# Hybrid attention and short-convolution layer: the last three product steps split by token block, one bias transfer and one power moved

## The chip, the cores and the metric

The kernel runs on one core of a Trainium2 chip. The metric is device time in microseconds (us), the median of three runs. Engines are named as in the profile: PE (matrix products) with PEld (its weight loads), DVE and ACT (elementwise), POOL (here powers and DMAs that add while they copy), SP (plain DMAs).

## The reference, cut to what matters

```python
h = rms_norm(x, norm_gain[i])
z = h @ w_in[i]                                  # q, k, v, gates, conv parts
...                                              # attention, short convolution
x = x + mix @ w_out[i]
gate = jax.nn.sigmoid(rms_norm(x, ple_gate_norm_gain[i]) @ w_ple_gate[i] + b_ple_gate[i])
e = rms_norm(p[i] @ w_ple_proj[i], ple_norm_gain[i])
x = x + gate * e
```

512 tokens, width 2048, all in float32. The change touches the end of the last line, the products of the gate before it, and two orders further ahead.

## The kernel before, in words

Almost every product is float32 made of two parts: `halves` (lines 198 to 200) splits an operand into a rounded part h (a cast on ACT, L199) and the rest l (a subtraction on DVE, L200), and a product is h by h, l by h and h by l. The seven large matrix products of the middle and the end (nine column groups of 1024) go by a scheme of seven instead of eight block products: sums of blocks of the weights (L185 to L191 on DVE, or L169 as an adding DMA from POOL) are multiplied with sums of blocks of the activations.

A group g has 28 steps (`PER`), listed in `steps`. A step (g, f, c) multiplies form f of the activations with one 128x2x512 piece of weights: 6 matmuls for token block t=0, then 6 for t=1 (`products`, called in `run_step`), each 128x128 by 128x512, into a PSUM accumulator "a", "b" or "c" that several forms share. In the last group (g=8) "a" is two single banks. Step numbers below count from 0 inside a group, so the last is 27. The split weights wh, wl live in three buffers: the cast for step s+3 can start when PE has left step s. PE runs its program in the order written; DVE, ACT, POOL and SP each run their own lists in order, and those lists come from two tables: `soon(before|after, step, fn)` in the grouped stages, and `at(tick, fn)` in the attention stage. An instruction that waits holds up all behind it on its engine.

In group 8 the last two steps were already reordered: t=0 of both, then `tail_work`, then t=1 of both (L246 to L254).

Three places matter here.

- **Attention stage** (125 to 263 us). `turn_q` transposes q and issues three small POOL DMAs (L810, L811, L813) that rearrange it for the scores matmuls (L829, L830, L832); the third waits for the first to land. `rstd_q` turns sums of squares into norms: one small DVE instruction (L585) and a power on POOL (L303). `take_e` stores e tiles (L913, POOL).
- **Group 1 into group 2** (350 to 370 us). `tap` multiplies a finished block z by a row of convolution weights (DVE, L1074) and stores it (POOL, L1075). Its z buffers are the four of the pool `quad`; group 2's first eviction (`first`, ACT, L320) takes one of them again, and the casts of group 2's weights are queued on ACT behind it.
- **Group 8** (822 us to the end), `gate_group(8)`. For a block (t, n) of 2x128 tokens by 512 columns: `take` copies the first accumulator, scaled, from PSUM (ACT, L1325); `add_b` adds the bias by a POOL DMA (L1328); `join` adds the second accumulator (DVE, L1333); then sigmoid (ACT, L1348), `times_e` (DVE, L1352), `add_x2` (POOL DMA, L1355) and `store`. Blocks (0,0) and (1,0) at the very end go by smaller pieces: `bias_first` puts the bias into PSUM ahead (L1340), `first_block` (L1431 and others) and `last_block` (L1422, L1412, L1416) finish them, with stores from SP (L1417).

```python
        if s == len(steps) - 2:
            tail_products.append(products)
            products(0)
        elif s == len(steps) - 1:
            products(0)
            for fn in tail_work:
                fn()
            tail_products[0](1)
            products(1)
```

Of the kernel before, what the change touches and what calls it, by code (L numbers as in the profile page):

```python
# [15 lines left out]
P = 128  # L16
T = 512
# [18 lines left out]
def hymba_layer(ctx: ExitStack, tc: tile.TileContext, io):  # L36
# [82 lines left out]
    def soon(table, s, fn, *args):  # L119
        table.setdefault(s, []).append((fn, args))  # L120
# [93 lines left out]
    def run_step(s, forms):  # L214
        g, f, c = steps[s]
        now[0] = s
        for fn, args in before.pop(s, ()):
            fn(*args)
        sums(s + (3 if g in LATE and s % PER < 8 else 4))
        prepare(s + 2)  # L220
        acc = {1: "a", 6: "a", 7: "a", 4: "a", 5: "b", 3: "b", 2: "c"}[f]
        start = f in (1, 5, 2)
        mine = [x for x in steps if x[:2] == (g, f)]
        first, last = c == mine[0][2], c == mine[-1][2]
        if start and first:
            if (g, acc) == (NG - 1, "a"):
                ps = [ps_t.tile([P, T], F32, name="pst") for _ in range(2)]
            else:
                ps = ps_abc[("abc".index(acc) + max(g - 1, 0)) % 3].tile([P, 2, T], F32, name="psp")
                if g >= NG - 2:  # L230
                    ps = [ps[:, b] for b in range(2)]
            psum[g, acc] = ps
        ps = psum[g, acc] if g >= NG - 2 else [psum[g, acc][:, b] for b in range(2)]
        wh, wl = weights[s]

        def products(t, f=f, c=c, wh=wh, wl=wl, first=first, last=last):
            for i in range(2):
                _, h, l = forms[2 * c + i][f]
                h, l = (a[:, t * P : (t + 1) * P] for a in (h, l))
                for n, (a, w) in enumerate(((h, wh), (l, wh), (h, wl))):  # L240
                    nc.tensor.matmul(  # L241
                        ps[t], a, w[:, i], start=start and first and i == 0 and n == 0,
                        stop=last and i == 1 and n == 2, skip_group_check=not start,
                    )

        if s == len(steps) - 2:  # L246
            tail_products.append(products)
            products(0)
        elif s == len(steps) - 1:
            products(0)  # L250
            for fn in tail_work:
                fn()
            tail_products[0](1)
            products(1)  # L254
        else:
            for t in range(2):
                products(t)
        if g in (0, 4, 6, 8):
            for i in range(2):
                for home in forms[2 * c + i][f][0]:  # L260
                    room[home] += 1
        while s in after:
            for fn, args in after.pop(s):
                fn(*args)
# [50 lines left out]
    def column(r, t, b):  # L315
        return r[:, 2 * t + b : 2 * t + b + 1]
# [288 lines left out]
    def rstd_q(t, n):  # L605
        blocks = slice(2 * t, 2 * t + 2)
        head_rstd(rq[t, n], eps_tok[:, blocks])
# [95 lines left out]
    def at(when, fn):  # L703
        later.append((when, len(later), fn))
# [28 lines left out]
    for b in range(NB):  # L733
        scale_k(b)

    for t in range(2):
        rope_q(t, 1)
        for b in range(2):
            at(9 + 2 * t + b, lambda t=t, b=b: square_q(t, 0, b, mtile))
        at(11 + 2 * t, lambda t=t: rstd_q(t, 0))  # L740
        at(14 + 3 * t, lambda t=t: rope_q(t, 0))
    mask = cw.tile([P, P], F32, name="mask", bufs=1)
    nc.gpsimd.dma_start(mask, io["mask"])
# [68 lines left out]
        turned[j, t, 0], turned[j, t, 1] = st, st2  # L812
        return lambda: nc.gpsimd.dma_start(st[HD:], low[:HD])  # L813

    turned, laid = {}, [None]

    def attention(j, n, when):

# [65 lines left out]

        if n % 2 == 0:
            at(when - 5, lambda: cell.update(last=turn_q(j, n // 2)))
            at(when - 4, lambda: cell["last"]())
        at(when, scores)
        at(when + 5, turn)
        at(when + 8, values)  # L890
# [160 lines left out]
    def square_group(g):  # L1051

        s0, q = g * PER, {}
        quarters(g, q, s0)

        def times(t, src):
            for b in range(2):
                stt(q[t, 0][:, b], src()[:, b], column(rx2_tok, t, b), q[t, 1][:, b], op0=ALU.mult, op1=ALU.mult)

        def last():  # L1060
            q[1, 0] = qtile("z")
            times(1, lambda: psum[g, "a"])

        taps = []

        def load_taps():
            for i in range(3):
                taps.append(itile("tap"))
                nc.sync.dma_start(taps[i], io["conv_rows"][i])

        def tap(i, t, home):

            out = q[home]
            tt(out, q[t, 0], taps[i].unsqueeze(1).broadcast_to([P, 2, T]), op=ALU.mult)  # L1074
            nc.gpsimd.dma_start(part(tap_dram[i].rearrange("(b p) n -> p b n", p=P), t, 0), out)  # L1075

        soon(after, s0 + 24, load_taps)
        soon(after, s0 + 27, times, 0, lambda: q[0, 0])
        soon(after, s0 + 28, last)
        for i, t, home, s in (  # L1080
            (2, 0, (0, 1), 28), (1, 0, (1, 1), 29), (0, 0, (0, 0), 30),
            (2, 1, (0, 1), 32), (1, 1, (0, 1), 36), (0, 1, (1, 0), 37),
        ):
            soon(after, s0 + s, tap, i, t, home)
# [228 lines left out]
    def gate_group(g):  # L1313
        s0 = g * PER
        q, ext = {}, {}

        def load_b(tile=itile):
            ext["b"] = tile("gb")
# [53 lines left out]
        soon(after, s0 + 13, add_b, 1, 1)  # L1372
        soon(before, s0 + 15, take, 0, 1, "a", n_2)
        soon(after, s0 + 15, load_e, 1, 1)
        soon(after, s0 + 16, join, 0, 1, "b", n_2)
        soon(after, s0 + 17, add_b, 0, 1)
        soon(after, s0 + 17, load_e, 0, 1)
        soon(before, s0 + 21, join, 1, 1, "a", n_2)
        finish(1, 1, s0 + 21, int(g == 7))
        finish(0, 1, s0 + 20)  # L1380

        def new_z():
            q[1, 0] = qtile("z")
# [30 lines left out]
        def add_and_store(t, n, b, cols=slice(0, T)):  # L1414
            z = q[t, n][:, b, cols]
            tt(z, z, ext["x2", t, n][b][:, cols], op=ALU.add)  # L1416
            nc.sync.dma_start(part(out, t, 2 + n)[:, b, cols], z)  # L1417

        def last_block():
            cols = [slice(h * T // 2, (h + 1) * T // 2) for h in range(2)]  # L1420
            for c in cols:
                nc.scalar.activation(  # L1422
                    q[1, 0][:, 1, c], psum[g, "a"][1][:, c], AF.Sigmoid, scale=column(r_2[0], 1, 1))
            for c in cols:
                times_scaled(1, 0, 1, c)
                add_and_store(1, 0, 1, c)

        def first_block():
            new_z()
            whole(1, 0, 0)  # L1430
            nc.scalar.activation(q[1, 0][:, 0], q[1, 0][:, 0], AF.Sigmoid)  # L1431
            add_and_store(0, 0, 1)
            times_scaled(1, 0, 0)
            add_and_store(1, 0, 0)

        soon(after, s0 + 15, load_b, spare)
        for i, fn in enumerate((load_x2, load_e)):
            for t in range(2):
                soon(after, s0 + 16 + 2 * i + t, fn, t, 0, *(spare,) * i)
        soon(before, s0 + 21, bias_first)  # L1440
        soon(after, s0 + 24, join, 0, 0, "c", r_2)
        for b in range(2):
# [2 lines left out]
            soon(after, s0 + 25, scale_e, t, 0, b)  # L1445
        soon(after, s0 + 25, times_e, 0, 0, 0)
        soon(after, s0 + 25, add_and_store, 0, 0, 0)
        soon(after, s0 + 25, times_scaled, 0, 0, 1)
        tail_work.append(first_block)
        soon(after, s0 + 27, last_block)  # L1450

    for g in T3_BY_DMA:
# [146 lines left out]
```

## Time and profile before

| | us |
|---|---|
| runs | 904.26, 904.36, 904.90 (median 904.36) |
| profiled execution, its own time | 905.72 |
| its span, first to last instruction | 904.0 |
| PE busy / DVE busy / ACT busy / POOL busy | 896.1 / 714.4 / 530.6 / 190.4 |
| granted TensorE clock, mean over the span | 0.999 of full speed |

The profiled execution is 1.36 us above the median of the runs; 1.72 us of it lie outside the span. The profile draws a 512-column matmul longer (0.39 us) than the time from one start to the next, since matmuls overlap: for the pace of PE the starts are to be read.

### The profile page before, as it was taken

How to read it: one execution, taken by the hardware profiler on the slowest of the kernel's cores; microseconds unless marked ns; L12 is line 12 of the kernel's file. 1: busy time of each engine (PE TensorE's matmuls, PEld its weight loads, DVE VectorE, ACT ScalarE, POOL GpSimd, SP SyncE). 2: the span in 40 equal slices, each digit the busy share in tenths (PEclk: the TensorE clock that was granted, in tenths of full speed). 3: DMA queues.
4: the chain of work that ended last, by engine and by line, in shares of the span. 5: the costliest groups of instructions: out<-in, count | busy, mean ns of one | idle time of the engine just before them, and what ended most of it. 6: DMA issues, size and time to landing. Idle time of an engine off the chain costs nothing.

```text
span 904.0 us, 11939 instructions
## 1 busy us (share of the span) xinstructions
PE 896.1 (99%) x4112; PEld 743.9 (82%) x4112; DVE 714.4 (79%) x974; ACT 530.6 (59%) x853; POOL 190.4 (21%) x264
## 2 busy tenths in 40 slices
PE   9999999999999999999999999999999999999997
PEld 7788888888888888888888888888888888888886
DVE  6878897978757687777678678997868887799678
ACT  7766856677744433454445458765656666665444
POOL 0323242656440002201130110002120122101100
PEclk9999999999999999999999999999999999999999
DMA  8999628666459769799488898849996995898775
GB/s 309 350 298 308 232 58 275 223 152 165 122 142 370 234 196 235 174 231 272 105 204 246 222 242 259 232 122 238 348 297 184 215 306 131 236 301 266 186 216 145
DMA packets 75612, 204.43 MB, mean 226 GB/s; under 512 B 9315, under 2 KB 16147, under 8 KB 75552
## 3 DMA queue, kind: packets, MB, share of 16 engines
q1 hardware_dynamic: 49392, 134.35, 42.9%
q0 software_dynamic: 26016, 69.31, 34.1%
q8 instruction: 32, 0.52, 0.2%
q14 instruction: 28, 0.23, 0.1%
q10 hardware_dynamic: 144, 0.01, 0.0%
HBM read 169.03 MB, written 33.56 MB: 224 GB/s over the span
## 4 chain that ended last, share of the span: by engine, by line
PE 95%; DVE 2%; issue 1%; DMA 1%; ACT 0%; SPq 0%; DVEq 0%; ACTq 0%
PE psp L241 70%; PE psg L725 8%; PE psp L531 5%; PE pst L241 3%; PE pst L1043 2%; PE pso L878 1%; PE pss L919 1%; PE pst L1475 1%; PE pst L919 1%; PE pst L861 1%; DVE wl L200 1%; PE pss L829 1%; PE pss L830 1%; DMA raw<-in_w_kv 0%; PE psm L806 0%
## 5 line engine op out<-in xcount | busy, mean ns | idle before, releaser
L241 PE MATMUL psp<-wh,form 128*128 128x512 f32 x1280 | 395.2, 390 | 0.0
L241 PEld LDWEIGHTS psp<-wh,form 128*128 128x128 f32 x1280 | 239.4, 188 | 49.0
L241 PE MATMUL psp<-wl,form 128*128 128x512 f32 x640 | 249.3, 389 | 0.2 <-DVE wl L200 0.2
L200 DVE TENSOR_TENSOR wl<-wy,wh 128x1024 fp32r<-128x1024 f32 x108 | 131.7, 1223 | 61.1 <-ACT wh L199 60.2
L199 ACT CAST wh<-wy 128x1024 fp32r<-128x1024 f32 x108 | 113.4, 1052 | 86.6 <-PE psp L241 69.0
L241 PEld LDWEIGHTS psp<-wl,form 128*128 128x128 f32 x640 | 120.1, 188 | 25.8 <-DVE wl L200 0.7
L200 DVE TENSOR_TENSOR wl<-wx,wh 128x1024 fp32r<-128x1024 f32 x72 | 87.9, 1224 | 51.3 <-ACT wh L199 51.2
L199 ACT CAST wh<-ws 128x1024 fp32r<-128x1024 f32 x72 | 75.9, 1055 | 73.9 <-PE psp L241 53.6
L241 PE MATMUL psp<-wh,hsh 128*128 128x512 f32 x304 | 118.7, 390 | 0.0
L199 ACT CAST wh<-wx 128x1024 fp32r<-128x1024 f32 x72 | 75.7, 1054 | 73.2 <-PE psp L241 52.6
L241 PE MATMUL psp<-wl,hsh 128*128 128x512 f32 x304 | 118.3, 389 | 0.0
L241 PE MATMUL psp<-wh,hsl 128*128 128x512 f32 x304 | 118.3, 389 | 0.0
L200 DVE TENSOR_TENSOR wl<-ws,wh 128x1024 fp32r<-128x1024 f32 x72 | 88.1, 1223 | 28.1 <-ACT wh L199 27.7
L189 DVE TENSOR_TENSOR wy<-wy,ws 128x1024 f32<-128x1024 f32 x72 | 87.7, 1219 | 0.0
L241 PEld LDWEIGHTS psp<-wl,hsh 128*128 128x128 f32 x304 | 57.1, 188 | 11.9
L241 PEld LDWEIGHTS psp<-wh,hsl 128*128 128x128 f32 x304 | 57.1, 188 | 11.8
L241 PEld LDWEIGHTS psp<-wh,hsh 128*128 128x128 f32 x304 | 57.1, 188 | 11.6
L725 PE MATMUL psg<-hsh,wh 128*128 128x512 f32 x112 | 45.0, 402 | 0.0
L169 POOL DMA_DIRECT2D wy<-in_w_mid x16 | 14.0, 877 | 143.4 <-DVE wy L189 81.3
L725 PE MATMUL psg<-hsh,wl 128*128 128x512 f32 x112 | 43.8, 391 | 0.0
L725 PE MATMUL psg<-hsl,wh 128*128 128x512 f32 x112 | 43.8, 391 | 0.0
L241 PE MATMUL pst<-wh,form 128*128 128x512 f32 x128 | 39.4, 389 | 0.0
(240 smaller groups left out, 1300.8 us busy)
## 6 DMA issues: line engine op xcount, KB each, us to landing
ws<-in_w_mid SPq DMA_DIRECT2D x40, 512.0 KB, 5.1
wx<-in_w_mid SPq DMA_DIRECT2D x24, 512.0 KB, 4.4
wy<-in_w_mid SPq DMA_DIRECT2D x20, 512.0 KB, 6.3
h<-form POOLq DMA_DIRECT2D x32, 256.0 KB, 6.2
wy<-in_w_mid POOLq DMA_DIRECT2D x16, 512.0 KB, 8.4
raw<-in_w_in SPq DMA_DIRECT2D x16, 512.0 KB, 4.2
wx<-in_w_out SPq DMA_DIRECT2D x16, 512.0 KB, 6.7
ws<-in_w_out SPq DMA_DIRECT2D x16, 512.0 KB, 5.9
```

The costliest lines, as they stand in the source:

```text
L169: nc.gpsimd.dma_start(t, w[n, r, j, c], accum_op=ALU.add)
L189: tt(y, y, got[g, "s1" if f == 6 else "s0", c], op=ALU.add)
L199: nc.scalar.copy(h, src)
L200: tt(l, src, f32(h), op=ALU.subtract)
L241: nc.tensor.matmul(ps[t], a, w[:, i], start=start and first and i == 0 and n == 0, stop=last and i == 1 and n == 2, skip_group_check=not s ...
L531: nc.tensor.matmul(kv_ps[t // 2][:, t % 2], hs[k][a][:, t * P : (t + 1) * P], kv_split[c][w][:, i], start=k == 0 and n == 0, stop=k == KT ...
L725: nc.tensor.matmul(ps, w[:, k % 8], a, start=k == 0 and n == 0, stop=k == KT - 1 and n == 2)
L829: nc.tensor.matmul(out, q, khh[j][:, ks], start=True, stop=False)
L830: nc.tensor.matmul(out, q, kll[j][:, ks], start=False, stop=True)
L861: nc.tensor.transpose(pt[:, r * P : (r + 1) * P], cell["t"][:, r], ident)
L919: nc.tensor.matmul(banks[t], a, w[:, k], start=k == 0 and i == 0, stop=k == 1 and i == 2)
L1043: nc.tensor.transpose(pt[:, b], quads[b // 2][:, b % 2, f * P : (f + 1) * P], ident)
```

## The change

Five edits.

1. The last three steps (25, 26, 27 of group 8) run t=0 of all three first. Then t=1 of all three for columns 0 to 255, into 256 columns of another PSUM bank ("side", its own accumulation), then t=1 for columns 256 to 511 into the old bank. 18 matmuls of 512 columns become 36 of 256, each with its own weight load.
2. The end of the last block is rewritten for it: ACT copies the scaled columns 0 to 255 of the old bank into z early; when "side" is complete, DVE adds it, and that half goes on to its store while PE does the other half. `add_and_store(0, 0, 1)` moves from `first_block` to behind the "side" work, `times_scaled(0, 0, 1)` to `begin_last`.
3. In group 8 the bias DMA of block (0,1) is issued after step 15, right behind its eviction, and `join` follows at step 17 (before: join 16, bias DMA 17); sigmoid and `times_e` of that block come two steps earlier.
4. In the attention stage the norms of the second pair of q's token blocks, for heads 0 to 7 (`rstd_q(1, 0)`), are listed at tick 15 instead of 13, and placed behind the last DMA of the second `turn_q`.
5. Two of the taps of group 1 are listed one step earlier.

```diff
-        def products(t, f=f, c=c, wh=wh, wl=wl, first=first, last=last):
+        def products(t, f=f, c=c, wh=wh, wl=wl, first=first, last=last, cols=slice(0, T), side=None, begin=False):
...
                 for n, (a, w) in enumerate(((h, wh), (l, wh), (h, wl))):
+                    at_first = begin or side is None and first and start
                     nc.tensor.matmul(
-                        ps[t], a, w[:, i], start=start and first and i == 0 and n == 0,
-                        stop=last and i == 1 and n == 2, skip_group_check=not start,
+                        ps[t][:, cols] if side is None else side, a, w[:, i, cols],
+                        start=at_first and i == 0 and n == 0, stop=last and i == 1 and n == 2,
+                        skip_group_check=not start and side is None,
                     )
-        if s == len(steps) - 2:
+        if len(steps) - 3 <= s < len(steps) - 1:
             tail_products.append(products)
             products(0)
         elif s == len(steps) - 1:
             products(0)
             for fn in tail_work:
                 fn()
-            tail_products[0](1)
-            products(1)
+            side = ps_abc[1].tile([P, 2, T], F32, name="psp")[:, 0, : T // 2]
+            psum[g, "side"] = side
+            for cols, home in ((slice(0, T // 2), side), (slice(T // 2, T), None)):
+                for i, fn in enumerate(tail_products + [products]):
+                    fn(1, cols=cols, side=home, begin=i == 0 and home is not None)
...
+    def late_rstd(t):
+        with tc.issue_after(moved[1].ins) if t else ExitStack():
+            rstd_q(t, 0)
+
...
-        at(11 + 2 * t, lambda t=t: rstd_q(t, 0))
+        at(11 + 4 * t, lambda t=t: late_rstd(t))
...
-            at(when - 4, lambda: cell["last"]())
+            at(when - 4, lambda: moved.append(cell["last"]()))
...
-            (2, 0, (0, 1), 28), (1, 0, (1, 1), 29), (0, 0, (0, 0), 30),
+            (2, 0, (0, 1), 28), (1, 0, (1, 1), 28), (0, 0, (0, 0), 29),
...
-        soon(after, s0 + 16, join, 0, 1, "b", n_2)
-        soon(after, s0 + 17, add_b, 0, 1)
+        soon(after, s0 + (17 if g == 7 else 15), add_b, 0, 1)
+        soon(after, s0 + (16 if g == 7 else 17), join, 0, 1, "b", n_2)
...
-        finish(0, 1, s0 + 20)
+        finish(0, 1, s0 + (20 if g == 7 else 18))
...
+        def begin_last():
+            new_z()
+            z = q[1, 0]
+            nc.scalar.activation(
+                z[:, 1, early], psum[g, "a"][1][:, early], AF.Copy, scale=column(r_2[0], 1, 1))
+            whole(1, 0, 0)
+            nc.scalar.activation(z[:, 0], z[:, 0], AF.Sigmoid)
+            times_scaled(0, 0, 1)
+            times_scaled(1, 0, 0)
+            add_and_store(1, 0, 0)
+
         def last_block():
-            cols = [slice(h * T // 2, (h + 1) * T // 2) for h in range(2)]
-            for c in cols:
-                nc.scalar.activation(
-                    q[1, 0][:, 1, c], psum[g, "a"][1][:, c], AF.Sigmoid, scale=column(r_2[0], 1, 1))
-            for c in cols:
+            z, r = q[1, 0][:, 1], column(r_2[0], 1, 1)
+            stt(z[:, early], psum[g, "side"], r, z[:, early], op0=ALU.mult, op1=ALU.add)
+            nc.scalar.activation(z[:, early], z[:, early], AF.Sigmoid)
+            nc.scalar.activation(z[:, late], psum[g, "a"][1][:, late], AF.Sigmoid, scale=r)
+            add_and_store(0, 0, 1)
+            for c in (early, late):
                 times_scaled(1, 0, 1, c)
                 add_and_store(1, 0, 1, c)
```

**How the order moves.** Line numbers of the changed kernel are 5 to 10 higher here (power L308, q's DMAs L819, L820, L822, tap L1083, join L1343, `times_e` L1362).

POOL in the attention stage, from the power of t=0 (msq_1681) on; st_1777, st_1778 and low_1779 are q of the second pair of token blocks. Before, then changed:

```order
L303 TENSOR_TENSOR msq_1681<-msq_1681,half_neg_175 128x16
L913 DMA e12_144<-e_1748 128x512
L303 TENSOR_TENSOR msq_1759<-msq_1759,half_neg_175 128x16
L810 DMA st_1778<-st_1777 64x512
L811 DMA st_1778<-low_1779 64x512
L913 DMA e03_141<-e_1802 128x512
L913 DMA e03_141<-e_1813 128x512
L813 DMA st_1777<-low_1779 64x512
```

```order
L308 TENSOR_TENSOR msq_1681<-msq_1681,half_neg_175 128x16
L922 DMA e12_144<-e_1748 128x512
L819 DMA st_1778<-st_1777 64x512
L820 DMA st_1778<-low_1779 64x512
L922 DMA e03_141<-e_1802 128x512
L922 DMA e03_141<-e_1813 128x512
L822 DMA st_1777<-low_1779 64x512
L922 DMA e13_145<-e_1824 128x512
L308 TENSOR_TENSOR msq_1759<-msq_1759,half_neg_175 128x16
```

The second power (msq_1759) goes from ahead of q's three DMAs to behind them and behind one store of e.

DVE at the start of group 2, the taps of group 1's block t=0 (z_3282 is the second one's output) among the weight splits. Before, then changed:

```order
L1074 TENSOR_TENSOR z_3426<-z_3196,tap_3623 128x1024
L200 TENSOR_TENSOR wl_3705<-wx_3490,wh_3704 128x1024
L1074 TENSOR_TENSOR z_3282<-z_3196,tap_3621 128x1024
L200 TENSOR_TENSOR wl_3723<-wy_3547,wh_3722 128x1024
L1074 TENSOR_TENSOR z_3196<-z_3196,tap_3619 128x1024
L200 TENSOR_TENSOR wl_3741<-wy_3568,wh_3740 128x1024
```

```order
L1083 TENSOR_TENSOR z_3426<-z_3196,tap_3623 128x1024
L1083 TENSOR_TENSOR z_3282<-z_3196,tap_3621 128x1024
L200 TENSOR_TENSOR wl_3707<-wx_3490,wh_3706 128x1024
L1083 TENSOR_TENSOR z_3196<-z_3196,tap_3619 128x1024
L200 TENSOR_TENSOR wl_3725<-wy_3547,wh_3724 128x1024
L200 TENSOR_TENSOR wl_3741<-wy_3568,wh_3740 128x1024
```

The second and third tap each pass one weight split; on POOL the second tap's store also passes the adding DMA of a weight block (wy_3630).

DVE in group 8, steps 16 to 23: z_7870 is block (0,1), z_7743 block (1,1), and the splits of steps 19 to 23 read wx_7350, wx_7377, ws0_7803, ws0_7838 and wy_7440. Before, then changed:

```order
L1333 SCALAR_TENSOR_TENSOR z_7870<-psp_7675,nr_x2_7043,z_7870 128x512 x2
L200 TENSOR_TENSOR wl_7924<-wx_7350,wh_7923 128x1024
L200 TENSOR_TENSOR wl_7949<-wx_7377,wh_7948 128x1024
L189 TENSOR_TENSOR wy_7440<-wy_7440,ws0_7768 128x1024
L200 TENSOR_TENSOR wl_7970<-ws0_7803,wh_7969 128x1024
L200 TENSOR_TENSOR wl_7990<-ws0_7838,wh_7989 128x1024
L1333 SCALAR_TENSOR_TENSOR z_7743<-pst_7590,nr_x2_7043,z_7743 128x512
L1333 SCALAR_TENSOR_TENSOR z_7743<-pst_7591,nr_x2_7043,z_7743 128x512
L1340 SCALAR_TENSOR_TENSOR pst_7591<-gb_7897,eps_tok_172,pst_7591 128x512
L189 TENSOR_TENSOR wy_7465<-wy_7465,ws0_7803 128x1024
L200 TENSOR_TENSOR wl_8011<-wy_7440,wh_8010 128x1024
L1352 SCALAR_TENSOR_TENSOR z_7870<-z_7870,r_e_6917,e_7940 128x512
```

```order
L200 TENSOR_TENSOR wl_7923<-wx_7350,wh_7922 128x1024
L1343 SCALAR_TENSOR_TENSOR z_7870<-psp_7675,nr_x2_7043,z_7870 128x512 x2
L200 TENSOR_TENSOR wl_7949<-wx_7377,wh_7948 128x1024
L189 TENSOR_TENSOR wy_7440<-wy_7440,ws0_7768 128x1024
L200 TENSOR_TENSOR wl_7971<-ws0_7803,wh_7970 128x1024
L1362 SCALAR_TENSOR_TENSOR z_7870<-z_7870,r_e_6917,e_7940 128x512
L1362 SCALAR_TENSOR_TENSOR z_7870<-z_7870,r_e_6917,e_7941 128x512
L200 TENSOR_TENSOR wl_7994<-ws0_7838,wh_7993 128x1024
L1343 SCALAR_TENSOR_TENSOR z_7743<-pst_7590,nr_x2_7043,z_7743 128x512
```

The join of (0,1) passes one split to the back and now stands behind the bias DMA in its data; the two products with e move from behind the split of step 23 to ahead of that of step 22.

## Rows read from the trace of the kernel before

**Rows 1.** Page, part 1: busy us (share of span) and instructions by engine.

```profile
PE 896.1 (99%) x4112; PEld 743.9 (82%) x4112; DVE 714.4 (79%) x974; ACT 530.6 (59%) x853; POOL 190.4 (21%) x264
```

**Rows 2.** Waits of PE over the span: us in total, times, longest.

```profile
PE pss L829 <- ACT wh L199: 0.3, 1, 0.3
PE psp L241 <- DVE wl L200: 0.2, 1, 0.2
```

**Rows 3.** Chain that ended last, in order of time: start, us, what.

```profile
822.33 10.88 PE pst L241 x48
```

**Rows 4.** Timeline of PE, attention stage: start, us, line, operation, tiles.

```profile
170.49 0.39 PE L725 MATMUL psg<-hsh,wl 128*128 128x512 f32 x1
...
170.96 0.28 PE L830 MATMUL pss<-khl,st 128*128 128x256 f32 x1
...
174.31 0.39 PE L725 MATMUL psg<-hsh,wl 128*128 128x512 f32 x1
...
175.18 0.28 PE L830 MATMUL pss<-khl,st 128*128 128x256 f32 x1
...
175.89 0.28 PE L830 MATMUL pss<-khl,st 128*128 128x256 f32 x1
```

**Rows 5.** Timeline of PE, group 2, step 6.

```profile
366.41 0.61 PE L241 MATMUL psp<-wh,form 128*128 128x512 f32 x2
...
367.61 0.62 PE L241 MATMUL psp<-wh,form 128*128 128x512 f32 x2
```

**Rows 6.** Timeline of PE, its last matmul.

```profile
898.12 0.39 PE L241 MATMUL pst<-wl,form 128*128 128x512 f32 x1
```

**Rows 7.** Timeline of DVE, group 8.

```profile
869.56 1.22 DVE L200 TENSOR_TENSOR wl<-wx,wh 128x1024 fp32r<-128x1024 f32 x1
...
878.77 1.47 DVE L1333 SCALAR_TENSOR_TENSOR z<-pst,nr_x,z 128x512 f32<-128x512 f32 x2
...
883.08 1.41 DVE L1352 SCALAR_TENSOR_TENSOR z<-z,r_e,e 128x512 f32<-128x512 f32 x2
...
892.72 1.22 DVE L200 TENSOR_TENSOR wl<-wy,wh 128x1024 fp32r<-128x1024 f32 x1
...
899.51 0.43 DVE L1416 TENSOR_TENSOR z<-z,xb 128x256 f32<-128x256 f32 x1
...
900.31 0.42 DVE L1416 TENSOR_TENSOR z<-z,xb 128x256 f32<-128x256 f32 x1
```

**Rows 8.** Timeline of POOL, attention stage.

```profile
165.05 2.93 POOL L303 TENSOR_TENSOR msq<-msq,half_neg 128x16 f32<-128x16 f32 x1
167.94 0.58 POOL L810 DMA_DIRECT2D st<-st  x1
...
170.85 0.53 POOL L813 DMA_DIRECT2D st<-low  x1 [0.70 <-DMA st<-st]
```

**Rows 9.** Line L813 at 170.85 alone: issue to landing.

```profile
DMA to landing us min/median/max: 4.0/4.0/4.0
```

**Rows 10.** Timelines of ACT and of POOL, start of group 2.

```profile
364.00 1.03 ACT L320 ACTIVATE z<-psp 128x1024 f32<-128x1024 f32 x1 [4.72 <-DMA t<-z]
...
357.41 0.74 POOL L1075 DMA_DIRECT2D t<-z  x1 [0.61 <-DVE z L1074]
```

**Rows 11.** Timelines of ACT, then of SP, group 8, steps 15 to 17.

```profile
863.17 0.69 ACT L1325 ACTIVATE z<-pst,nr_x 128x512 f32<-128x512 f32 x1 [0.67 <-PE pst L241]
...
868.83 0.99 SPq L1345 DMA_DIRECT2D e<-e  x2
```

**Rows 12.** Issue to landing: all six bias DMAs (L1328); then the two at 868.83.

```profile
DMA to landing us min/median/max: 7.2/10.0/13.0
...
DMA to landing us min/median/max: 6.8/7.5/8.2
```

**Rows 13.** DMA issues after 840 us: count, KB each, us to landing.

```profile
z<-x POOLq DMA_DIRECT2D x2, 512.0 KB, 5.4
```

**Rows 14.** Busy time by stretch: PE, PEld, DVE, ACT, POOL, clock, DMA share, GB/s.

```profile
864.00:866.00 2.00, 2.00 (x11) 1.65 (x10) 1.17 (x2) 1.09 (x2) 0.00 (x0) 1.00 0.00 0
```

More of the change, by code (lines that the diff above doesn't have):

```diff
@@ L813, in turn_q @@
         return lambda: nc.gpsimd.dma_start(st[HD:], low[:HD])
-    turned, laid = {}, [None]
+    turned, laid, moved = {}, [None], []
     def attention(j, n, when):
@@ L1315, in gate_group @@
         q, ext = {}, {}
+        early, late = slice(0, T // 2), slice(T // 2, T)
         def load_b(tile=itile):
@@ L1417, in add_and_store @@
             nc.sync.dma_start(part(out, t, 2 + n)[:, b, cols], z)
-        def last_block():
-            cols = [slice(h * T // 2, (h + 1) * T // 2) for h in range(2)]
-            for c in cols:
-                nc.scalar.activation(
-                    q[1, 0][:, 1, c], psum[g, "a"][1][:, c], AF.Sigmoid, scale=column(r_2[0], 1, 1))
-            for c in cols:
+        def begin_last():
[8 more added lines that the diff above has]
+            add_and_store(1, 0, 0)
+        def last_block():
+            z, r = q[1, 0][:, 1], column(r_2[0], 1, 1)
[4 more added lines that the diff above has]
+            for c in (early, late):
                 times_scaled(1, 0, 1, c)
                 add_and_store(1, 0, 1, c)
[L1428 to L1434, printed above, removed]
         soon(after, s0 + 15, load_b, spare)
-        for i, fn in enumerate((load_x2, load_e)):
-            for t in range(2):
-                soon(after, s0 + 16 + 2 * i + t, fn, t, 0, *(spare,) * i)
+        for t in range(2):
+            soon(after, s0 + 16 + t, load_x2, t, 0)
+            soon(after, s0 + 18 + t, load_e, t, 0, spare)
         soon(before, s0 + 21, bias_first)
@@ L1447, in gate_group @@
         soon(after, s0 + 25, add_and_store, 0, 0, 0)
-        soon(after, s0 + 25, times_scaled, 0, 0, 1)
-        tail_work.append(first_block)
+        tail_work.append(begin_last)
         soon(after, s0 + 27, last_block)
```

## Prediction

> **What bounds the kernel now.** The busy times come first: PE is at work for 99% of the span, DVE for 79% [rows 1], so only three kinds of time are to be had: the head, the few stalls of PE, and what comes behind its last matmul. The waits of PE name two stalls in mid-kernel, and put them at 0.3 and 0.2 us [rows 2]. Since matmuls are drawn longer than their pace, I measure them by starts. The chain of waits gives the pace: 48 matmuls of 512 columns in 10.88 us, 0.2267 us each [rows 3], a step of 12 in 2.72. In the attention stage the second matmul of a scores group follows the last of the projection by 0.47 us where nothing is late (170.49 to 170.96), and by 0.87 at 174.31 to 175.18 [rows 4]: 0.40 us lost. In group 2 three matmuls from 366.41 take until 367.61 instead of 0.68 us [rows 5]: 0.52 lost. At the end the last matmul is drawn to 898.51 (898.12 + 0.39) [rows 6], and the last addition ends at 900.73 [rows 7]: 2.22 us of drain ahead of the final store.
>
> **Edit 4, the power.** POOL works on the second power for 2.93 us from 165.05; only then, at 167.94, does it issue the first of q's three DMAs, and the third at 170.85, when the first has landed [rows 8]. The third lands 4.0 us later [rows 9], at 174.85, which is where PE goes on. Without the power ahead of it the first goes out at about 165.1, the third 2.9 us earlier, and lands at about 172, 2.5 us before PE asks. Gain 0.40. The power itself is not saved: it now stands ahead of one store of e, which waited for it before as well, and its norms belong to heads 0 to 7, whose scores come last. The bounds are 0 (another releaser) and 0.40.
>
> **Edit 5, the taps.** ACT's eviction for group 2 starts at 364.00, after 4.72 us of waiting for the store of the second tap, issued at 357.41, 6.6 us before [rows 10]. Behind it stand the casts, behind those the splits. The second tap passes one split of about 1.22 us [rows 7], so its store goes out at about 356.2, now ahead of the adding DMA. If it takes its 6.6 us again it lands at 362.8, and cast and split are 1.2 us earlier: more than the 0.52 they lacked. Sooner than the end of step 3 (366.41 - 2 x 2.72 = 360.97) the eviction can't start in any case. Gain 0.52; bounds 0 and 0.52. What it costs: the split of step 3 comes one tap later. Its buffer is free two steps ahead of its use, 5.4 us, and cast, two taps and split take about four times 1.22 = 4.9, so it is hidden, by little. The adding DMA that is passed feeds step 7, one step behind the stalled one.
>
> **Edits 1 and 2, the end.** First the matmuls. The nearest row has the same size: from 175.18 to 175.89, six starts of 256-column matmuls, each with its own weight load, are 0.118 us apart [rows 4]. 36 x 0.118 = 4.25 against 18 x 0.2267 = 4.08: 0.17 lost. Then the drain. Before, ACT and DVE do two halves after the last matmul; the first half's addition ends at 899.94 (899.51 + 0.43), the second's at 900.73 [rows 7]. Now one half is left: 0.79 gained, 0.62 net. The early half must be out of the way: after "side" is complete 18 x 0.118 = 2.1 us of matmuls remain, then about half a us of sigmoid, while DVE has four 256-column instructions of 0.43 and one of twice the width: 2.6 us at most. That fits, barely. The 19th of the 36 waits for ACT's early copy, which has 2.1 us from the end of t=0. Bounds: 0.2 (the early half in the way by one addition) and 0.79.
>
> The three orders t=0 also ask for the last splits sooner. The first matmul of step 25 was at 898.12 - 35 x 0.2267 = 890.19. The split of step 27 is first read by the third matmul of that step, before the 21st from there (894.72), now the 15th (893.36). It was done at 893.94 (892.72 + 1.22) [rows 7]. So by itself edit 1 makes PE wait 0.6 us, 0.7 with the weight load.
>
> **Edit 3, the bias.** This is what pays for that. DVE runs without a gap from 878.77 to the end of that split, and the two products with e, 1.3 us from 883.08 to the next instruction [rows 7], leave that stretch for an earlier place. Whether there is room depends on two landings. First the bias: ACT's eviction ends at 863.86 [rows 11], POOL can issue at about 864.2, and DVE reaches the join at 870.8, behind the split of step 19 [rows 7]. So the DMA has 6.6 us. The six bias DMAs took 7.2 to 13.0 [rows 12], the same kind of adding DMA at a quiet time 5.4 [rows 13]; and from 864 to 866 nothing moves at all [rows 14]. I take 6.5, near the quiet end: no wait. Second the e tiles: issued at 868.83 to 869.8 [rows 11], the second landing 8.2 us after its issue [rows 12], at about 877.5. Then product 0.7, split of step 22 1.2: 879.4, while DVE began the join of (1,1) at 878.77 [rows 7]. About 0.65 of the 1.3 is lost again, and the split of step 27 ends at 893.94 - 1.3 + 0.65 = 893.3, within 0.1 of its need at 893.36. I take 0 for this, between 0 and 0.7 for landings like these; later ones are a rival.
>
> **Sum.** 0.40 + 0.52 + 0.62 = 1.54 us. The profiled execution has 904.0 of span and 905.72 in all: 904.18 would come of it. The median of the runs, 1.36 lower, goes from 904.36 to **902.82**. Of the time that is 0.17%, just under the 0.2% (1.8 us) that a measurement of this kernel can tell from no change.
>
> **Rivals.** *DVE is held up in front of the bias.* A late bias now stops every split behind the join. At the median of the six, 10.0 us, it lands at 874.2, 3.4 us after DVE got there. Following the list with these durations, the splits of steps 23, 25 and 27 come 0.8, 0.3 and 1.1 us late: 2.2 in all, 905.0, slower than before. It decides from a landing 7.5 us after the issue on, loses the whole gain at about 9.3, is slower by over 0.2% from about 11; at 13.0 it would be 908. For it: none of the six took less than 7.2 [rows 12]. Against it: the empty DMA queues [rows 14]. Chance 0.16, of which 0.05 beyond 0.2%.
>
> *The two middle stalls stay.* The profile puts the first down to an ACT cast [rows 2], not to the DMA that I inferred, and PE's lead may be lost at the next late thing. Then only the end is gained: 904.36 - 0.62 = 903.7. Against it: the landing at 174.85 fits the start to 0.1 us, and no other wait of PE is listed behind these [rows 2]. Chance 0.14.
>
> *The weight loads don't hide behind half-length matmuls.* A load takes 743.9 / 4112 = 0.18 us on average [rows 1]; 36 of them in a row with their matmuls would add 6.5 us: 909.3. Rows 4 speak against it: seven such pairs at 0.118 each. [...] Chance 0.02.
>
> **How the numbers follow.** My forecast has 0.68, with a range of its own from 902.2 (all upper bounds, and a quicker store) to 903.4 (the 0.6 of edit 1 only half covered). Under 902.55 (faster by over 0.2%) lies about a third of it, 0.22. Over 906.17 lie 0.05 of the first rival and the third, 0.07. The rest, 0.71, is within 0.2%. The range from 902.1 to 904.7 takes in the forecast, the second rival and the milder part of the first.
>
> **What would show it.** Right: no wait of PE at the scores line, q's first DMA at about 165.1; no wait on the split in group 2, and ACT's eviction there before 363; 36 matmuls 0.118 apart; 1.4 us from the last matmul's end to the last addition; a span of about 902.5. The bias lands less than 7 us after its issue, and the split of step 27 ends within 0.1 of its first reader. Wrong: a DVE gap over 2 us ahead of the join of (0,1), or waits of PE on splits in the last five steps; a wait of PE on ACT in the middle of the 36; the same middle stalls with another releaser.

## The result, and the profile after

The changed kernel takes 903.48 us, median of 22 runs (902.96 to 905.04), beside 904.51 for the kernel before in the same runs (903.94 to 908.25). The medians are 1.03 us apart. The ratio of the runs, which is an estimate of its own and not the quotient of the medians, is 0.9985, 95% interval 0.9978 to 0.9992: 1.4 us less, between 0.7 and 2.0. That is inside the 0.2% which the prediction named as the limit of a measurement here, so "within 0.2%" and the range 902.1 to 904.7 held, with 902.8 some 0.7 below the median. The range takes in the median of the kernel before as well, so the time by itself says little for the mechanism; the traces have to.

The profiled execution took 903.04 us, its span is 901.3, 2.7 less than before: more than the runs gained. The page of the changed kernel: busy time, share of the span and instructions of each engine, then the chain that ended last by engine:

```profile
PE 895.8 (99%) x4130; PEld 745.5 (83%) x4130; DVE 716.0 (79%) x975; ACT 530.8 (59%) x854; POOL 192.0 (21%) x264
...
PE 99%; DMA 0%; DVE 0%; ACT 0%; SPq 0%; issue 0%
```

PE is as busy as in [rows 1]. Of its waits (us in total, times, longest), those of [rows 2] are gone; one in the head is left:

```profile
PE pst L372 <- PEq L1594: 0.8, 1, 0.8
```

**Attention stage.** POOL's timeline (start, us, line, operation, tiles, idle time before and who ended it): q's three DMAs (L819, L820, L822) now stand ahead of the second power (L308); in [rows 8] the first stood behind it at 167.94 and the third at 170.85.

```profile
163.06 0.53 POOL L819 DMA_DIRECT2D st<-st  x1 [0.66 <-ACT st L199]
164.44 0.52 POOL L820 DMA_DIRECT2D st<-low  x1 [0.85 <-DVE low L200]
...
166.18 0.54 POOL L822 DMA_DIRECT2D st<-low  x1
...
167.29 3.19 POOL L308 TENSOR_TENSOR msq<-msq,half_neg 128x16 f32<-128x16 f32 x1
```

The same two steps of PE as in [rows 4]: the last of a projection, then scores.

```profile
169.76 0.39 PE L730 MATMUL psg<-hsh,wl 128*128 128x512 f32 x1
169.99 0.28 PE L838 MATMUL pss<-khl,st 128*128 128x256 f32 x1
170.10 0.28 PE L839 MATMUL pss<-khl,st 128*128 128x256 f32 x1
...
173.46 0.39 PE L730 MATMUL psg<-hsh,wl 128*128 128x512 f32 x1
173.69 0.28 PE L838 MATMUL pss<-khl,st 128*128 128x256 f32 x1
```

Nothing is lost at either: 0.34 us from the projection to the second scores matmul at 170.10. In [rows 4] the first of the two took 0.47, which I had read as undisturbed.

**Group 2.** ACT's eviction and the first cast behind it. In [rows 10] the eviction was released by a DMA after 4.72 us; now PE releases it:

```profile
359.80 1.03 ACT L325 ACTIVATE z<-psp 128x1024 f32<-128x1024 f32 x1 [1.89 <-PE psp L242]
360.72 1.04 ACT L199 CAST wh<-wy 128x1024 fp32r<-128x1024 f32 x1
```

**Group 8, the bias.** POOL issues it behind ACT's second copy:

```profile
862.22 0.86 POOL L1338 DMA_DIRECT2D z<-in_b_ple_gate  x1 [16.61 <-ACT z L1335]
```

and the view of line L1338 at that place alone has its time from issue to landing:

```profile
DMA to landing us min/median/max: 5.3/5.3/5.3
```

It lands at 867.5. DVE comes to the join (L1343) 1.2 us later, without a gap behind the split. The two products with e follow at 874.20, and the last row is the split of step 27:

```profile
867.58 1.23 DVE L200 TENSOR_TENSOR wl<-wx,wh 128x1024 fp32r<-128x1024 f32 x1 [1.19 <-ACT wh L199]
868.72 1.41 DVE L1343 SCALAR_TENSOR_TENSOR z<-psp,nr_x,z 128x512 f32<-128x512 f32 x2
...
874.20 1.45 DVE L1362 SCALAR_TENSOR_TENSOR z<-z,r_e,e 128x512 f32<-128x512 f32 x2
...
889.76 1.22 DVE L200 TENSOR_TENSOR wl<-wy,wh 128x1024 fp32r<-128x1024 f32 x1
```

It ends at 890.98. PE's timeline has its first reader at 891.41, and behind it the first of the 36 short matmuls, three starts in 0.36 us:

```profile
891.41 0.39 PE L242 MATMUL pst<-wl,form 128*128 128x512 f32 x1
...
892.31 0.40 PE L242 MATMUL psp<-wh,form 128*128 128x256 f32 x2
892.55 0.28 PE L242 MATMUL psp<-wl,form 128*128 128x256 f32 x1
892.67 0.40 PE L242 MATMUL psp<-wh,form 128*128 128x256 f32 x2
```

**The end.** PE's last 256-column matmul, ACT's last sigmoid, DVE's last product and addition, beside [rows 6] and the last of [rows 7]:

```profile
896.51 0.28 PE L242 MATMUL pst<-wl,form 128*128 128x256 f32 x1
...
896.82 0.47 ACT L1444 ACTIVATE z<-pst,r_x 128x256 f32<-128x256 f32 x1 [0.59 <-PE pst L242]
...
897.33 0.42 DVE L1422 TENSOR_TENSOR z<-z,e 128x256 f32<-128x256 f32 x1 [0.15 <-ACT z L1444]
897.79 0.42 DVE L1426 TENSOR_TENSOR z<-z,xb 128x256 f32<-128x256 f32 x1
```

From the last matmul's drawn end (896.79) to the end of the last addition (898.21) are 1.42 us, for 2.22 before; this stretch is called the drain below.

**Where the 2.7 us are.** I count starts of PE's matmuls, which stand in the same order in both kernels up to group 8. "Head" goes to the start of the 746th (where the scores in question begin; no edit acts before). The loss at the scores is the time from the 746th to the 776th less 5.43, its least value in any profile; the loss in group 2 is the time from the 1701st to the 1713th less 12 x 0.2267; the end goes from the 4003rd to the end of the span. What lies between these is equal in all profiles within 0.09 us.

| | head | scores | group 2 | end | span |
|---|---|---|---|---|---|
| before | 169.58 | 0.65 | 0.54 | 30.59 | 904.0 |
| after | 168.85 | 0.00 | 0.00 | 29.87 | 901.3 |
| difference | 0.73 | 0.65 | 0.54 | 0.72 | 2.7 |

0.73 of it no edit made: in the profiles of this study heads lie from 168.70 to 170.71.

### The profile page after: what moved, and what is told of

Its sections match the earlier page's. It is cut to its first block, busy times and chain, and to the rows that moved or that the text cites. A ratio compares the mean times of both kernels' runs of the same rounds, so it can differ in the third digit from the quotient of the medians.

```text
span 901.3 us, 11980 instructions
## 1 busy us (share of the span) xinstructions
PE 895.8 (99%) x4130; PEld 745.5 (83%) x4130; DVE 716.0 (79%) x975; ACT 530.8 (59%) x854; POOL 192.0 (21%) x264
## 4 chain that ended last, share of the span: by engine, by line
PE 99%; DMA 0%; DVE 0%; ACT 0%; SPq 0%; issue 0%
PE psp L242 72%; PE psg L730 9%; PE psp L536 5%; PE pst L242 5%; PE pst L1052 2%; PE pso L887 1%; PE pss L928 1%; PE pst L1488 1%; PE pst L928 1%; PE pst L870 1%; PE pss L839 1%; PE pss L838 1%; PE psm L815 0%; DMA x<-in_x 0%; PE pss L841 0%; PE psm L765 0%
## 5 line engine op out<-in xcount | busy, mean ns | idle before, releaser
L242 PE MATMUL psp<-wh,form 128*128 128x512 f32 (+1 forms) x1292 | 397.4, 389 | 0.0
L242 PEld LDWEIGHTS psp<-wh,hsl 128*128 128x128 f32 x304 | 57.1, 188 | 11.7
L242 PE MATMUL pst<-wh,form 128*128 128x512 f32 (+1 forms) x128 | 37.9, 379 | 0.0
```

The source lines that it names most:

```text
L242: nc.tensor.matmul(ps[t][:, cols] if side is None else side, a, w[:, i, cols], start=at_first and i == 0 and n == 0, stop=last and i == 1 ...
```

## The experiments

The first four take one edit each from the kernel before.

**Edits 1 and 2 alone.** The diff is that of the change for `run_step`, `begin_last` and `last_block`, with `add_b`, `finish`, `tap` and `rstd_q` as before.

> The kernel before with edits 1 and 2 alone (three steps' t=0 first, then 36 matmuls of 256 columns, the first half in a bank of its own); the power, the taps and the bias stay as before. Theory: the last splits are asked for sooner, and without edit 3 DVE has no room: PE waits about 0.6 to 0.7 us for the split of step 27, close ahead of the 36 matmuls. These take 36 x 0.120 = 4.3 us, the drain from the last matmul's end to the last addition falls from 2.22 to 1.4 us, and the two cancel: the span is that of the kernel before within 0.3 us. The middle stalls (0.87 for 0.34 at the scores, 0.52 in group 2) are still there. Rival: DVE has the room anyway and PE waits for nothing; then the span is 0.6 us shorter, and edit 3 was worth nothing.

904.69 us, ratio 0.9999 (0.9990 to 1.0007). PE's timeline ahead of the 36:

```profile
891.57 0.61 PE L242 MATMUL pst<-wh,form 128*128 128x512 f32 x2
892.66 0.50 PE L242 MATMUL pst<-wl,form 128*128 128x512 f32 x1 [0.47 <-DVE wl L200]
```

Three starts take 1.43 us (891.57 to the next step at 893.00) instead of 0.68: 0.75 lost at step 27's split. Its drain is 1.42. The end is 30.78, 0.2 longer than before: the halves alone gain nothing.

**Edit 4 alone.**

```diff
-        at(11 + 2 * t, lambda t=t: rstd_q(t, 0))
+        at(11 + 4 * t, lambda t=t: late_rstd(t))
```

> The kernel before with edit 4 alone (the second power on POOL behind q's third DMA). Theory: both of the steps ahead of the scores fall to the 0.34 us of a start that nothing delays (they were 0.47 and 0.87), so 0.5 to 0.66 us go, no wait of PE at the scores line is listed, and the drain is 2.22 as before. Since PE then reaches group 2 earlier, the stall there may grow by as much as is gained if the eviction behind the second tap's store does not move with PE: then the stall in group 2 is 0.5 to 1.2 us instead of 0.52. Rival: another releaser takes the place of the DMA, and PE goes on as late as before.

904.09 us, ratio 0.9998 (0.9989 to 1.0006). Loss at the scores 0.00. The stall in group 2 did not grow: only 0.03 was lost, though the tap's store was still what released ACT's eviction. That was not in my theory of a fixed 0.52.

**Edit 5 alone.**

```diff
-            (2, 0, (0, 1), 28), (1, 0, (1, 1), 29), (0, 0, (0, 0), 30),
+            (2, 0, (0, 1), 28), (1, 0, (1, 1), 28), (0, 0, (0, 0), 29),
```

> The kernel before with edit 5 alone (the second and third tap one step earlier). Theory: ACT's eviction in group 2 is released by PE and no longer by the store of a tap, starts 1.3 us or more earlier as measured against PE, and the stall of 0.52 us in group 2 is gone; the stall at the scores (0.87 for 0.34) stays; span 0.5 us shorter. Rival: PE's place in group 2 is held by something else, and nothing is gained.

904.16 us, ratio 1.0001 (0.9992 to 1.0009). No loss in group 2; the loss at the scores is 0.49, and the profile names the DMA here, where [rows 2] had named an ACT cast:

```profile
174.19 0.36 PE L829 MATMUL pss<-khl,st 128*128 128x256 f32 x1 [0.25 <-DMA st<-low]
```

**Edit 3 alone.**

```diff
-        soon(after, s0 + 16, join, 0, 1, "b", n_2)
-        soon(after, s0 + 17, add_b, 0, 1)
+        soon(after, s0 + (17 if g == 7 else 15), add_b, 0, 1)
+        soon(after, s0 + (16 if g == 7 else 17), join, 0, 1, "b", n_2)
...
-        finish(0, 1, s0 + 20)
+        finish(0, 1, s0 + (20 if g == 7 else 18))
```

> The kernel before with edit 3 alone (in group 8 the bias of block (0,1) by the adding DMA right behind ACT's eviction, its join behind that, its sigmoid and products two steps earlier). The matmuls of the end and the drain stay as before. Theory: the bias lands 5 to 6.5 us after its issue and ahead of the join, DVE waits for nothing there, the split of step 27 ends 0.7 to 1.3 us earlier against PE's first matmul of that step, and the time does not change (within 0.2 us): by itself the edit buys only room. Rival (DVE held up): the bias lands 7.5 us or more after the issue, DVE stands still ahead of the join for over 1 us, and PE waits for splits behind it.

904.46 us, ratio 1.0000 (0.9991 to 1.0009), end 30.58 as before. The bias lands 5.2 us after its issue. The split of step 27:

```profile
890.84 1.22 DVE L200 TENSOR_TENSOR wl<-wy,wh 128x1024 fp32r<-128x1024 f32 x1
```

It ends at 892.06 with PE's last start at 897.25, 5.19 apart; before it was 893.94 and 898.12, 4.18 apart [rows 6, 7]. So the edit buys 1.0 us of room and by itself no time.

**The kernel before once more, and the end without the middle.** The first is unchanged; the second is the changed kernel with edits 4 and 5 undone.

> The kernel before, unchanged, for a second profile and for the spread of a ratio that must be 1. Theory (the middle stalls are a matter of landings): PE's stall at the scores is somewhere from 0.1 to 0.7 us and the one in group 2 from 0 to 0.5, not the 0.40 and 0.52 of the first profile, and the group 2 stall is there only if the second tap's store lands more than 6.0 us after its issue; the drain is 2.22 us. Rival (fixed costs): 0.5 and 0.5 again, within 0.05.

> The kernel before with edits 1, 2 and 3 (everything in group 8), without 4 and 5. Theory: the end gains what it gains in the changed kernel: no wait of PE in the last ten steps, 1.42 us of drain and a store that ends 3.1 us behind it, 0.6 to 0.8 us in all; the two middle stalls are as in the kernel before, and they come and go with landings: the scores lose 0.1 to 0.7 us, because q's third DMA is issued behind the power, and group 2 between 0 and 0.5, something only when the tap's store lands more than 6.0 us after its issue. So the median lies 0.3 to 0.7 us above the changed kernel's. Rival (the middle is worth nothing): the median is the changed kernel's within 0.1 us.

The first: 904.45 us, ratio 1.0000 (0.9991 to 1.0009), which is what eleven runs can resolve: 0.8 us either way. The second: 903.56, ratio 0.9991 (0.9982 to 1.0000). By the traces the theory holds, and neither stall is a fixed cost. The six profiles without edit 4 and the six without edit 5 (issue and landing from the line's own view, starts of PE and losses from the starts):

| no edit 4 | third DMA of q issued, lands after | landed | PE free | lost |
|---|---|---|---|---|
| before once more | 167.99, 5.3 | 173.3 | 173.54 | 0.00 |
| edits 1 and 2 | 168.23, 5.4 | 173.6 | 173.68 | 0.21 |
| edit 5 | 168.31, 5.7 | 174.0 | 173.78 | 0.49 |
| edits 1 to 3 | 168.42, 5.9 | 174.3 | 174.04 | 0.51 |
| before | 170.85, 4.0 | 174.9 | 174.54 | 0.65 |
| edit 3 | 169.14, 5.3 | 174.4 | 173.96 | 0.74 |

| no edit 5 | tap's store lands after | lost in group 2 |
|---|---|---|
| edit 4; edits 1 to 3; edit 3 | 6.0 | 0.03, 0.09, 0.09 |
| before once more | 6.1 | 0.14 |
| edits 1 and 2 | 6.3 | 0.36 |
| before | 6.5 | 0.54 |

In the rows with a loss at the scores, what is lost is what the landing (issue plus landing time) is later than PE, and 0.23 to 0.34 us more. The means are 0.43 and 0.21. In every profile with edit 4 (eight) the loss at the scores is 0.00 to 0.03, in every one with edit 5 (eight) that in group 2 is 0.00. Edit 4 does not always leave much room, though: in the profile of the one-bank run below, q's third DMA waited until 167.93 for the first to land, took 5.8 us, and landed only 0.2 us before PE was free. The runs, however, don't show what the two stalls cost: with the end alone the median is within 0.1 us of the changed kernel's, as the rival said, where the traces would have 0.6; by the ratios (0.9991 and 0.9985) it is 0.5. All of these fit an interval of 0.8 us; how often the two stalls occur among runs is open.

**Edit 3 undone.** The changed kernel with the two lines above as they were.

> The changed kernel with edit 3 undone (bias by DMA behind step 17, join at 16, products at 21 and 22, as in the kernel before). Theory: DVE has no room for the earlier need of step 27's split, PE waits for it as it did with edits 1 and 2 alone (0.83 us between two starts over the pace there), both middle stalls stay away, drain 1.4 us: the span is 0.7 to 0.9 us longer than that of the changed kernel for the same head, the median about 904.2. Rival: without the middle stalls PE, and with it every landing, stands elsewhere, the room is there, and nothing is lost.

904.25 us, ratio 0.9992 (0.9983 to 1.0001); the end is 30.64, 0.77 longer than after. The wait of edits 1 and 2 is back:

```profile
892.30 0.50 PE L242 MATMUL pst<-wl,form 128*128 128x512 f32 x1 [0.45 <-DVE wl L200]
```

**The bias held back.** Ahead of the DMA in `add_b`, for block (0,1) of group 8, with one power, then two:

```diff
+                nc.gpsimd.tensor_tensor(spin, some, some, op=ALU.mult)
+                nc.gpsimd.tensor_tensor(spin, spin, half_neg[:, :16], op=ALU.pow)
             nc.gpsimd.dma_start(q[t, n], io["b_ple_gate"][2 * (g - 7) + n], accum_op=ALU.add)
```

> The changed kernel with one power of 128x16 and one small product on POOL between ACT's eviction of block (0,1) and its bias DMA in group 8 (their results are not used): the DMA is issued about 3.5 us later. Theory (a late bias stops DVE's list): it lands 5.3 us after its issue, about 8.8 us after the issue without this, 2.3 us after DVE got to the join. Followed through the splits behind it (room 1.6 us at step 25, 0.4 at step 27, and 0.5 to 0.7 of idle time of DVE ahead of them), PE waits 1.1 to 1.2 us in the last three steps, and the span is about 1.2 us longer; the threshold lies at a landing 7.7 us after the undelayed issue. Rival: the landing is hidden by DVE's other work, the list has more room than the steps say, and nothing is lost.

> The same with two powers: the DMA is issued about 6.5 us later and lands about 11.8 us after the undelayed issue. Theory: each us behind the threshold costs a us, so 4.1 to 4.3 us of waits of PE on splits and a span 4.2 us longer than the changed kernel's, 906.5 to 907.7. Rival: hidden, nothing lost; or the cost grows faster than the delay, since a late split also gives its buffers back late, and the span is over 6 us longer.

907.61 us (five runs, ratio 1.0036) and 911.78 (four runs, 1.0079): more than expected, because the landings themselves grew. One power: the DMA on POOL's timeline, and the join with its wait on DVE's.

```profile
865.60 0.92 POOL L1344 DMA_DIRECT2D z<-in_b_ple_gate  x1
...
874.08 1.41 DVE L1349 SCALAR_TENSOR_TENSOR z<-psp,nr_x,z 128x512 f32<-128x512 f32 x2 [4.88 <-DMA z<-in_b_ple_gate]
```

Its landing (the line's own view), then PE's waits:

```profile
DMA to landing us min/median/max: 8.5/8.5/8.5
```

```profile
PE pst L242 <- DVE wl L200: 2.1, 3, 1.0
```

Two powers: the DMA goes out at 871.02 and lands 8.8 us later. The join on DVE's timeline, and PE's waits:

```profile
879.82 1.41 DVE L1349 SCALAR_TENSOR_TENSOR z<-psp,nr_x,z 128x512 f32<-128x512 f32 x2 [9.10 <-DMA z<-in_b_ple_gate]
```

```profile
PE pst L242 <- DVE wl L200: 5.3, 1, 5.3
```

Measured from where POOL was released (862.40, 863.93), the bias lands after 11.7 and 15.9 us, and the ends are 3.56 and 7.87 us longer than after (33.43, 37.73). A line through these two points has a slope of 1.03 and reaches zero at 8.2 us. So the mechanism of the first rival is real and costs about a us for a us, and the changed kernel, at 5.3, stands some 2.9 us from it; two points make the line, and nothing was measured between about 5.3 and 11.7. That the landing itself grew goes with busier queues: in the changed kernel the DMA starts while the 16 engines are busy for 0.36 of the stretch, with one power it starts among SP's loads. No run changes the loads alone, so that these are the cause is not shown. First row the changed kernel, 862 to 864; second, of the other, 866 to 868 (the number before the last is the DMA share):

```profile
862.00:864.00 2.00, 2.00 (x11) 1.65 (x10) 1.11 (x1) 1.09 (x2) 0.86 (x1) 1.00 0.36 31
```

```profile
866.00:868.00 2.00, 2.00 (x10) 1.66 (x9) 0.81 (x2) 1.05 (x1) 0.51 (x1) 1.00 1.01 322
```

**One bank instead of two.** The changed kernel with t=1 of the last three steps at 512 columns:

```diff
-            for cols, home in ((slice(0, T // 2), side), (slice(T // 2, T), None)):
-                for i, fn in enumerate(tail_products + [products]):
-                    fn(1, cols=cols, side=home, begin=i == 0 and home is not None)
+            for fn in tail_products + [products]:
+                fn(1)
```

> The changed kernel with the last three steps' t=1 as 18 matmuls of 512 columns in one bank instead of 36 of 256 in two; the two sigmoids and their products then all stand behind the last matmul, as before the change. Theory: the 18 take 4.08 us against 36 x 0.120 = 4.30, 0.2 less, and the drain from the last matmul's end to the last addition is 2.2 us again instead of 1.42: net 0.6 us longer than the changed kernel. Rival: the drain is hidden elsewhere (the last store waits for something else) and the time is the same, or shorter by 0.2.

904.07 us, ratio 0.9995 (0.9986 to 1.0003); the end is 30.42, 0.56 longer than after. Both sigmoids are behind the last matmul again, and so are four DVE instructions, of which this is the last:

```profile
896.88 0.84 ACT L1438 ACTIVATE z<-pst,r_x 128x256 f32<-128x256 f32 x2 [2.66 <-PE pst L242]
...
898.64 0.42 DVE L1423 TENSOR_TENSOR z<-z,xb 128x256 f32<-128x256 f32 x1
```

The drain is 2.22 us (896.84 to 899.06).

**Other cuts.** 384 and 128 columns; then 320 and 192, with one addition moved to POOL:

```diff
-        early, late = slice(0, T // 2), slice(T // 2, T)
+        early, late = slice(0, 320), slice(320, T)
...
-            add_and_store(0, 0, 1)
+            z0 = q[0, 0][:, 1]
+            nc.gpsimd.tensor_tensor(z0, z0, ext["x2", 0, 0][1], op=ALU.add)
+            nc.sync.dma_start(part(out, 0, 2)[:, 1], z0)
```

> The changed kernel with the last three steps' t=1 cut into 384 and 128 columns instead of 256 and 256. From the two sizes measured (512 in 0.2267, 256 in 0.120 us) a start costs 0.013 us and a column 0.417 ns: 384 columns 0.173, 128 columns 0.067 us, if the weight load hides. Theory: it hides at 256 and still nearly at 128: 18 x 0.173 = 3.1 us, then 18 x 0.067 to 0.12, 1.2 to 2.2 us. Rival (a load is what a short matmul waits for): the 18 short ones take as long as those of 256 columns, 0.12 each, 2.2 us, or longer, as long as a load of 0.18 us each, 3.2 us. The first part's work (a sum, a sigmoid, two additions of DVE) no longer fits behind it, so the drain is longer than a quarter's own work: 1.5 to 2.2 us.

> The changed kernel with the cut at 320 columns, so that 192 are left for the drain, and with the addition of x2 to block (0,0) that DVE does just ahead of the drain moved to POOL, which is idle there. Theory: 18 x (0.147 + 0.093) = 4.3 us, as before; sigmoid 0.45 and the two DVE instructions 0.35 each: drain 1.2 instead of 1.42, and DVE is done with the first part in time. The span is 0.2 us shorter, which the trace shows and the runs hardly can. Rival: 192 columns are not faster than 256, or DVE is late with the first part, and nothing is gained, or up to 0.5 us lost.

The first, one run: 903.49 us, end 30.10, 0.23 longer than after. Its drain is only 1.05 us, shorter than I expected, but its 128-column matmuls are no faster than this (five intervals from 896.98 to 897.53; the last rows of PE's timeline):

```profile
896.98 0.39 PE L242 MATMUL pst<-wh,form 128*128 128x128 f32 x2
897.20 0.28 PE L242 MATMUL pst<-wl,form 128*128 128x128 f32 x1
897.31 0.39 PE L242 MATMUL pst<-wh,form 128*128 128x128 f32 x2
897.53 0.27 PE L242 MATMUL pst<-wl,form 128*128 128x128 f32 x1
```

0.111 each: the rival was nearer. The 384-column ones take 0.175.

The second: 904.20 us, ratio 0.9997 (0.9989 to 1.0006), end 30.77, a loss of 0.9. 192 columns take 0.111, no less than 128; and DVE was late beside POOL's addition (timelines of DVE and POOL):

```profile
895.02 2.61 DVE L1422 TENSOR_TENSOR z<-z,e 128x512 f32<-128x512 f32 x2
...
895.79 1.29 POOL L1446 TENSOR_TENSOR z<-z,xb 128x512 f32<-128x512 f32 x1 [7.10 <-DVE z L1422]
```

The two products take 1.48 us in the changed kernel. Neither cut beats it, and no version here does.

## Why the prediction was right, and where its sum was off

The total was 1.54 us; the runs have 1.4 by their ratio (0.7 to 2.0) and 1.03 between the medians. The traces have 1.26 on average: 0.43 at the scores, 0.21 in group 2, and 0.62 at the end (30.56 in five profiles of the old end, 29.94 in the two with edits 1 to 3 and no other cut or delay; 0.72 in the pair). The mechanism held at all three places; one term, edit 5, was priced more than twice too high.

**Edit 4**, forecast 0.40, bounds 0 and 0.40. The mechanism is as told: q's first DMA went out at 163.06 (165.1 was forecast), no wait is left, and the DMA, not the cast that the profile named, was the releaser. The upper bound was wrong: in the pair of profiles 0.65 was lost, in another 0.74, because the 0.47 taken for undisturbed had 0.13 of delay in it, which was missed at both steps. The times themselves were a draw: in the other five profiles without edit 4 the second power ran at 162.3 to 162.8 instead of 165.05 [rows 8], the third DMA went out 1.7 to 2.9 us earlier, and it landed after 5.3 to 5.9 us instead of 4.0 [rows 9].

**Edit 5**, forecast 0.52. The step that failed is the price: "Gain 0.52" is the profiled execution's loss (0.54 by the count above), which ran 1.36 us above the median, and I took it off the median. Five other profiles lose 0.03 to 0.36. ACT's eviction now waits for PE alone, and is well ahead of the forecast 363.

**Edits 1 and 2**, forecast 0.62. The drain came as forecast (1.42 for 1.43). From the first of the 36 matmuls (892.31) to the last's drawn end are 4.48 us, where 18 whole ones take 17 x 0.2267 + 0.39 = 4.24: 0.24 lost instead of 0.17, in part since the pace was 0.120 instead of 0.118. Net 0.56, which the one-bank run shows by itself; most of the other 0.16 of the pair's 0.72 is the way from the last addition to the end of the span (3.25 before, 3.12 after), which spreads by as much among profiles of one end.

**Edit 3**, forecast as what pays for 0.6 to 0.7 us of waiting. Shown from both sides: without it 0.75 and 0.77 are lost, with it nothing. The landing was 5.3 us, not 6.5, and the split of step 27 ended 0.43 us ahead of its reader, not within 0.1. What was off there is the price of the second landing: of the 1.3 us, 0.65 were to be lost again to the e tiles, and edit 3 alone kept 1.0. In the changed kernel the tiles are issued at 867.20 and 867.83 and land after 6.9 to 7.0 us, at 874.1 and 874.8, and the first product starts at 874.20, the second right behind it. So it is the e tiles, not the bias, that came with no room to spare.

**Rivals.** DVE held up by the bias: did not happen at 5.3 us, but is there, from 8.2 us on (7.5 was forecast), and at 13.0 the measured line gives 4.9 us lost where 5.2 were forecast. The middle stalls stay: wrong in the traces; the runs alone could not have refuted it. The loads don't hide: wrong at 256 columns, where a pair takes 0.120 us; (0.2267 - 0.120) / 256 is 0.417 ns a column, so its columns alone are 0.107. Below that it may hold: 128 and 192 columns both take 0.111 us, so of the sizes tried no pair takes less. That the load is what sets this 0.111 is not shown. Of the three cuts tried, the one at half costs the least time on PE.

## What to carry to other kernels

One profile's stall is one draw: before it is taken off a median, look how far that execution stood above the median, and profile the kernel again. The two waits here that end with a DMA's landing cost 0.00 to 0.74 us at the scores and 0.03 to 0.54 us in group 2 from one profile to another, so moving the issue ahead gains only the mean of what was lost (0.43 and 0.21); how much room is left has to be read from several profiles too. Halving the last matmuls paid here only where what feeds them, a split three places up DVE's list, was early enough for the new order: without edit 3 PE lost 0.75 and 0.77 us at it.

## What the runs showed of the hardware

A 512 KB adding DMA (the bias) that went out right behind its eviction landed 5.3 us after its issue in the changed kernel and 5.2 with edit 3 alone, and 8.5 and 8.8 where it was issued 3.2 and 7.1 us later among SP's loads. The DMA share in the stretch of 2 us behind the issue was 0.81 and 0.57 in the first two (864 to 866), 1.01 and 0.99 in the others (866 to 868, 872 to 874).

While POOL did a 128x512 addition (1.29 us from 895.79), one DVE product of 128x512 took 1.83 us; the one before it took 0.68, and without that addition the same two take 0.68 and 0.69 in the changed kernel. That is one product in one profile, and what in the addition made it longer is not shown.

With two powers ahead of the bias PE stood still for 5.25 us; in the 4.6 us behind that 0.50 of full speed was granted, and the 512-column pace was 0.427 us instead of 0.2267. The row gives the stretch, its length, PE's busy us, the granted clock, the DMA share and GB/s:

```profile
882.40:887.00 4.60, 4.58 (x11) 0.50 0.02 5
```

In the same kernel DVE's list was almost as late: it ran without a gap from 879.82, and its split of step 27 ended 0.3 us ahead of its reader. So the slow stretch can account for at most 0.3 us of that run's loss.
